# A hybrid decoder layer: where the rotary tables, the decays' sums, one row of the merged block and a few small steps stand

## The chip, the cores and the metric

The kernel runs on one core of one Trainium2 chip. The metric is the time of one execution on the device in microseconds; lower is better. The core has five engines with instruction queues of their own: TensorE multiplies matrices, VectorE and GpSimd do elementwise work, ScalarE does activations and copies, and SyncE (SP) only issues transfers here. Each engine takes its instructions strictly in order. Data lies in DRAM, in the on-chip SBUF (128 partitions), and, for the results of matmuls, in the banks of PSUM.

## The reference

One layer for 1024 tokens of width 1024, in float32: a norm, one wide projection, two token mixers side by side, their merge by gates, an output projection, a residual and a last norm.

```python
h = rms_norm(x, norm_w[layer])
proj = jnp.einsum('btd,de->bte', h, w_in[layer])
(a_q, a_k, a_v, a_gate, b_q, b_k, b_v, b_gate, b_low, m_a, m_b) = jnp.split(proj, offsets, axis=-1)

q = rope(a_q.reshape(bsz, t, A_HEADS, A_HEAD_DIM), positions)
k = rope(a_k.reshape(bsz, t, A_KV_HEADS, A_HEAD_DIM), positions)
v = a_v.reshape(bsz, t, A_KV_HEADS, A_HEAD_DIM)
o_a = sliding_window_attention(q, k, v, a_sinks[layer]) * jax.nn.silu(a_gate)
y_a = jnp.einsum('bte,ed->btd', o_a, w_a_proj[layer])

gk = jnp.einsum('btr,re->bte', b_low, b_gate_up[layer]) + b_gate_bias[layer]
log_a = jax.nn.log_sigmoid(gk.astype(jnp.float32)) / GATE_TAU
o_b = gated_linear_attention(b_q, b_k, b_v, log_a)
o_b = rms_norm(o_b, b_out_norm_w[layer]) * jax.nn.silu(b_gate)
y_b = jnp.einsum('bte,ed->btd', o_b, w_b_proj[layer])

merged = jax.nn.sigmoid(m_a) * y_a + jax.nn.sigmoid(m_b) * y_b
x = x + jnp.einsum('btd,de->bte', merged, w_out[layer])
return rms_norm(x, final_norm_w)
```

`rope` turns the first 32 and the last 32 columns of a head by angles position x frequency, and so needs a table of sines and one of cosines. `gated_linear_attention` multiplies queries by exp(b) and keys by exp(-b), where b is the running sum of `log_a` within a chunk.

## The kernel before

**Precision.** Every matmul operand is split into a high part (a cast to a shorter float format, on ScalarE) and a low part (the difference, on VectorE or GpSimd), and each product is made of three matmuls. For weights this is `split_w` (L116 to L118): `wh` on ScalarE, `wl` on the engine named by `rest[0]`, GpSimd for most of the kernel and VectorE at the start and at the end.

**Seven products.** The large projections use a scheme with seven half-size products in place of eight: `seven_products` (L455). It takes sums of weight blocks (L467 to L470, VectorE) and sums of the activations' blocks, which are made once: `tr` holds the raw sums t1 to t4 (L233 to L239), and `t_split` (L287) splits them (L292 on ScalarE, L293 on VectorE). The products' results are added up on VectorE (L489, L506, L531), and a function `emit` handles each finished block.

**The order of the work.** (1) `token_tile` loads a tile of 128 tokens, sums squares on ScalarE (L214), forms the scale on GpSimd (`rstd_of`, L144: L146 multiplies by 1/n and adds the epsilon, L147 raises to the power -0.5), applies scale and norm weights on VectorE (L220; the weights lie in two PSUM banks `nwb`, filled by a matmul with ones, L208), and transposes on TensorE with the identity `ident` (L224). (2) Four projections of the gate `m_a` (`m_half`, `m_tiles`, L250 and L332) and the rank-16 projection `low` (L355 to L365). (3) `pair` (L598) runs `seven_products` over pairs of column blocks: four pairs for `m_b`, each followed by `log_gate` (L576) for one head, then for the two halves of the heads the pairs for q and k of the linear attention, then its gate and its values. `log_gate` forms the running sums of the decays for one head and half of the tokens: three activations on ScalarE, and a minimum, a difference, a scan, a copy and a difference on VectorE; the result `gx` goes to DRAM (`sp_cum`, L595). When q and k are finished, `keep` (L616) loads that block back (L629), takes its exponential on ScalarE (L630) and multiplies on GpSimd (L631). The tiles for this come alternately from the pools `mwork` and `ex`, of two buffers each. (4) Window attention over 8 pairs of heads. (5) Linear attention (`gla`). (6) The projection of the first mixer (`ya`). (7) The projection of the second mixer, again as seven products, with the merge of the gates in `merge` (L1084), and the split of the merged blocks for the last projection in `sums` (L1051). (8) The output projection, the residual and the last norm (`norm`, `finish`).

**The rotary tables.** `rotary_tables` (L383) is a chain of 33 instructions on VectorE over tiles of 128 x 256 that reduces the angles to a turn, two sines on ScalarE (L420) and twelve stores to DRAM (L424). It is called behind the second pair of `m_b` and its log gates, with `issue_after(scan)`, which puts its VectorE instructions behind that scan.

**The merged blocks.** `mg` holds the merged blocks: c11, c12, c21 and c22 are its quarters, four rows (index k) of 128 x 512 each. The output projection's first product uses `mt[0]`, the split of c21, and so needs c21's row 3, which becomes ready with the sixth product of the last of four rounds (k = 3). `sums(6)` splits that row, then forms the sum row 3 (`sum_row(3)`: t1s = c22 - c21) and splits it into `mt[5]`. The merge of a block takes two loads and two VectorE instructions (L1090, L1091).

**What sets the order.** The program is written in the order above, and a planner that simulates the engines in time gives each engine its queue: of the instructions that it holds ready it takes the one that stands earliest in the text. `issue_after` adds a lower bound, `high_priority(offset=n)` puts what is under it n places earlier. Pools on the right side of SBUF are a stack: a pool that is opened after another was closed takes the same place and waits for the readers of what lay there.

## Time and profile before

| what | us |
|---|---|
| three timed runs | 1079.79, 1079.21, 1076.34 (median 1079.21) |
| the profiled execution | 1076.43 |
| its span, first to last instruction | 1074.6 |
| TensorE busy | 1027.0 (96%) |
| VectorE busy | 756.3 (70%) |
| ScalarE busy | 540.8 (50%) |
| GpSimd busy | 507.3 (47%) |
| moved by DMA | 140.54 MB, mean 131 GB/s |

The profile is of one execution. Busy time of TensorE counts the time in which a matmul was under way, at whatever clock; whether it keeps its pace is seen from the number of matmuls in a stretch. Idle time is put down to whatever released the engine last.

### The profile page before, as it was taken

What the parts mean: (1) busy time and instruction counts of PE and PEld (TensorE: products, weight loads), DVE (VectorE), ACT (ScalarE), POOL (GpSimd) and SP (SyncE); (2) the same over time, 40 slices, a digit from 0 to 9 for tenths busy, and PEclk for the clock granted to TensorE, in tenths of its full rate; (3) what the DMA queues carried; (4) which work ended last, traced back from release to release, by engine and by line L of the source; (5) the groups of instructions that cost most, each with busy time, mean ns of one, the idle gap of its engine ahead of it and who ended that gap; (6) DMA issues with size and microseconds to landing.
All of it is one profiled execution on the core that took longest, in us unless ns stands there. A gap on an engine that the chain in (4) does not pass through costs nothing.

```text
span 1074.6 us, 16232 instructions
## 1 busy us (share of the span) xinstructions
PE 1027.0 (96%) x5572; PEld 872.0 (81%) x5572; DVE 756.3 (70%) x1315; ACT 540.8 (50%) x1321; POOL 507.3 (47%) x438
## 2 busy tenths in 40 slices
PE   7999998989999999999999999989989999997996
PEld 5788866867889998888888888878778887786996
DVE  6984797444665332379988787878856388899786
ACT  6535576333343223466766667647655244244445
POOL 3034444778897444766678676747843100000002
PEclk9999999989999999999999999999999999999999
DMA  8413343444333317222222222429764388442415
GB/s 275 113 59 108 128 137 123 153 141 136 101 109 108 118 40 216 59 59 59 71 59 59 78 71 76 140 84 303 244 222 158 115 268 256 136 140 97 167 52 194
DMA packets 126260, 140.54 MB, mean 131 GB/s; under 512 B 10337, under 2 KB 87009, under 8 KB 126178
## 3 DMA queue, kind: packets, MB, share of 16 engines
q1 hardware_dynamic: 126178, 139.51, 41.1%
q8 instruction: 44, 0.72, 0.3%
q14 instruction: 38, 0.31, 0.1%
HBM read 94.52 MB, written 40.24 MB: 125 GB/s over the span
## 4 chain that ended last, share of the span: by engine, by line
PE 61%; DVE 9%; POOL 2%; ACT 2%; issue 2%; DMA 2%; SPq 0%; POOLq 0%; DVEq 0%; ACTq 0%
PE pj L134 25%; PE sj L134 13%; PE sj L452 13%; PE sc L765 2%; PE av L805 2%; PE av L849 2%; PE pt L789 1%; DVE b L978 1%; PE sc L849 1%; PE av L889 1%; DMA oraw<-sp_oa 1%; PE av L890 1%; PE pt L922 1%; DVE wl L118 1%; DVE sm L788 1%
## 5 line engine op out<-in xcount | busy, mean ns | idle before, releaser
L134 PE MATMUL pj<-o,wh 128*128 128x512 f32 x1072 | 348.2, 399 | 2.2 <-DVE o L228 1.6
L134 PEld LDWEIGHTS pj<-o,wh 128*128 128x128 f32 x1072 | 198.7, 190 | 42.9 <-DVE o L228 2.0
L134 PE MATMUL pj<-o,wl 128*128 128x512 f32 x536 | 213.2, 398 | 0.0
L118 POOL TENSOR_TENSOR wl<-sraw,wh 128x512 fp32r<-128x512 f32 (+1 forms) x98 | 155.5, 1604 | 111.8 <-ACT wh L117 105.1
L134 PEld LDWEIGHTS pj<-o,wl 128*128 128x128 f32 x536 | 101.1, 189 | 21.0
L134 PE MATMUL sj<-o,wh 128*128 128x512 f32 x352 | 111.2, 395 | 1.6 <-DVE o L489 0.8
L117 ACT CAST wh<-wr 128x1024 fp32r<-128x1024 f32 (+1 forms) x76 | 66.4, 890 | 78.4 <-PE sj L452 22.4
L117 ACT CAST wh<-sraw 128x512 fp32r<-128x512 f32 (+1 forms) x98 | 63.4, 678 | 83.7 <-PE sj L134 22.4
L146 POOL TENSOR_SCALAR rstd<-zs 128x1 f32<-128x1 f32 x8 | 2.7, 334 | 210.1 <-DVE zs L1110 209.7
L118 POOL TENSOR_TENSOR wl<-wr,wh 128x1024 fp32r<-128x1024 f32 x26 | 64.1, 2467 | 66.4 <-ACT wh L117 66.4
L506 DVE TENSOR_TENSOR u<-u,sj 128x512 f32<-128x512 f32 x48 | 32.9, 685 | 68.8 <-PE sj L134 35.6
L134 PEld LDWEIGHTS sj<-o,wh 128*128 128x128 f32 x352 | 65.7, 187 | 18.2 <-ACT u L515 1.3
L134 PE MATMUL sj<-o,wl 128*128 128x512 f32 x176 | 69.4, 394 | 0.0
L452 PE MATMUL sj<-wh,b 128*128 128x256 f32 x320 | 60.8, 291 | 6.0 <-DVE b L978 4.2
L134 PE MATMUL sj<-t,wh 128*128 128x512 f32 x144 | 57.6, 400 | 0.0
L489 DVE TENSOR_TENSOR c<-u,sj 128x512 f32<-128x512 f32 x48 | 32.7, 682 | 34.9 <-PE sj L134 10.5
L452 PEld LDWEIGHTS sj<-wh,b 128*128 128x128 f32 x320 | 51.8, 199 | 6.7 <-DVE b L978 4.4
L452 PE MATMUL sj<-wh,o 128*128 128x256 f32 x320 | 55.9, 278 | 1.3 <-DVE o L569 1.3
L780 ACT ACTIVATE sm<-sc,nm 128x129 f32<-128x129 f32 x128 | 45.8, 369 | 22.5 <-DVE nm L776 22.1
L797 POOL TENSOR_TENSOR ch<-ph,cst 128x512 fp32r<-128x512 f32 x32 | 37.1, 1158 | 40.4 <-ACT ph L796 32.9
L118 DVE TENSOR_TENSOR wl<-wr,wh 128x512 fp32r<-128x512 f32 (+1 forms) x50 | 45.4, 924 | 14.3 <-ACT wh L117 14.2
L452 PEld LDWEIGHTS sj<-wh,o 128*128 128x128 f32 x320 | 48.8, 188 | 1.6 <-DVE o L569 1.5
(316 smaller groups left out, 2707.0 us busy)
## 6 DMA issues: line engine op xcount, KB each, us to landing
sraw<-in_w_in_dram SPq DMA_DIRECT2D x32, 512.0 KB, 3.9
wr<-in_w_in_dram SPq DMA_DIRECT2D x26, 512.0 KB, 3.9
r<-sp_ob SPq DMA_DIRECT2D x28, 256.0 KB, 4.3
qs<-q SPq DMA_DIRECT2D x72, 64.0 KB, 2.0
xt<-in_x_dram SPq DMA_DIRECT2D x8, 512.0 KB, 8.1
sp_ma<-gt SPq DMA_DIRECT2D x16, 256.0 KB, 2.4
sp_mb<-c SPq DMA_DIRECT2D x16, 256.0 KB, 2.0
gt<-sp_cum SPq DMA_DIRECT2D x16, 256.0 KB, 3.4
```

What stands on the lines that cost most here:

```text
L117: nc.scalar.copy(h, raw)
L118: rest[0].tensor_sub(l, raw, h.bitcast(F32))
L134: nc.tensor.matmul(p, a[:, k, :], b[:, k, :], start=start and k == 0 and y == 0, skip_group_check=True, stop=stop and k == 3 and y == 2)
L452: nc.tensor.matmul(p, m[i][:, k, t * P : t * P + P], w[j][:, k, :], start=start and k == 0 and y == 0, skip_group_check=True, stop=stop an ...
L489: nc.vector.tensor_add(o, like(u[i][b], o), like(x[j][b], o))
L506: nc.vector.tensor_add(o[b], u[i][b], x[j][b])
L765: nc.tensor.matmul(s[:, h * 256 : h * 256 + 256], lq, kk[kv][x][:, k0 : k0 + 2, :].rearrange("p n t -> p (n t)"), start=x == 0, stop=x == 1)
L780: nc.scalar.activation(sm[:, j, :], sel[j // 2][:, j % 2, :], AF.Exp, bias=nm[:, j : j + 1], accum_out=den[:, j : j + 1])
L788: nc.vector.tensor_scalar_mul(sm[:, j, :P], sm[:, j, :P], den[:, j : j + 1])
L797: nc.gpsimd.tensor_mul(ch, ph.bitcast(F32), leb)
L805: nc.tensor.matmul(av[:, b * 256 : b * 256 + 256], val[:, blk, kv, :], part[:, 2 * b : 2 * b + 2, :], start=y == 0, stop=y == len(terms) - 1)
L849: nc.tensor.matmul(p, a[i], b[j], start=start and y == 0, stop=stop and y == 2)
```

## The change

Six edits:

1. `rotary_tables` is called right behind the splits of the t blocks and the last `m_a` tile, ahead of the pairs; `issue_after` puts its VectorE instructions behind the last split. Its pool `rt` moves from `gctx` to `tctx`, which closes there.
2. The decays' sums stay in SBUF: four tiles `cum` of 128 x 1024 take the place of the DRAM tile `sp_cum`. The eight stores and sixteen loads go, and so does the pool `ex`; the exponential reads `cum` and writes a tile of `mwork`.
3. In the last round of the second mixer's projection the merge and the split of c21's row 3 get a priority 400 places earlier; the merge of c22's row 3 is put off until behind that split, and the splits of c12 are put behind it as well.
4. The mean and the epsilon move out of `rstd_of`: the square takes a scale of D to the power -0.5, and the epsilon enters the sum as an extra column (of `xt` and of `ssq`). The first and the last norm so have one GpSimd instruction less for each tile; the linear attention's norm keeps it.
5. The norm weights and the identity are loaded through ScalarE's queue.
6. `low` is made ahead of the second halves of the first three `m_a` tiles and ahead of the t splits; the mask `caus` becomes a view of `le`, without the cast.

```diff
-    sp_cum = spill.tile([BH * BK, T], F32, name="sp_cum")
...
-    def rstd_of(pool, ss, n, width):
-        r = pool.tile([P, width], F32, name="rstd")
-        nc.gpsimd.tensor_scalar(r, ss, 1.0 / n, EPS, ALU.mult, ALU.add)
-        nc.gpsimd.tensor_tensor(r, r, mhalf[:, :width], ALU.pow)
+    def power(pool, ss):
+        r = pool.tile([P, 1], F32, name="rstd")
+        nc.gpsimd.tensor_tensor(r, ss, mhalf, ALU.pow)
         return r
...
-    rt = gctx.enter_context(pool_of(name="rt", bufs=1, side="right"))
...
     tctx = ExitStack()
+    rt = tctx.enter_context(pool_of(name="rt", bufs=1, side="right"))
     td = tctx.enter_context(pool_of(name="td", bufs=1, side="right"))
...
-        xts = [xp1.tile([P, D], F32, name=f"xt{t}") for t in range(NT)]
+        xts = [xp1.tile([P, D + 1], F32, name=f"xt{t}") for t in range(NT)]
+
+        for xt in xts:
+            nc.gpsimd.memset(xt[:, D:], (EPS * D) ** 0.5)
...
         load(0)
-        nc.sync.dma_start(cst[:, :P], consts[:, :P])
-        nc.sync.dma_start(nwr, norm_w)
+        nc.scalar.dma_start(nwr, norm_w)
+        nc.scalar.dma_start(cst[:, :P], consts[:, :P])
         load(1)
...
-            nc.scalar.activation(junk, xt, AF.Square, accum_out=ss)
-            r = rstd_of(xp, ss, D, 1)
+            nc.scalar.activation(junk, xt, AF.Square, scale=D**-0.5, accum_out=ss)
+            r = power(xp, ss)
...
+    last_split = []
...
-            nc.vector.tensor_sub(m[1][:, k, :], r[:, k, :], f(m, 0, k))
+            last_split.append(nc.vector.tensor_sub(m[1][:, k, :], r[:, k, :], f(m, 0, k)).ins)
...
-    for c in range(3):
-        m_half(c, w_first[c], 1)
-    t4, t2, t3, t1 = (t_split(*y) for y in ((4, None), (2, "t4"), (3, "t2"), (1, "t3")))
     low = lp.tile([P, T], F32R, name="low")
...
-    caus = const.tile([P, P], I32, name="caus")
-    nc.vector.tensor_copy(caus, le)
+    for c in range(3):
+        m_half(c, w_first[c], 1)
+    t4, t2, t3, t1 = (t_split(*y) for y in ((4, None), (2, "t4"), (3, "t2"), (1, "t3")))
+    caus = le.bitcast(I32)
...
     m_tiles([3])
-    rctx.close()
-    tctx.close()
-    c1.close()
...
+    with tc.issue_after(last_split[-1]):
+        rotary_tables()
+    rctx.close()
+    tctx.close()
+    c1.close()
...
-    decays = [mwork, sctx.enter_context(pool_of(name="ex", bufs=2))]
+    cums = gctx.enter_context(pool_of(name="cum", bufs=1, side="right"))
+    cum = [cums.tile([P, T], F32, name=f"cum{i}") for i in range(BH)]
...
-        gx = up_.tile([P, 512], F32, name="u3")
+        gx = cum[hd][:, sl]
...
-        nc.sync.dma_start(sp_cum[hd * BK : hd * BK + BK, sl], gx)
-        return scan.ins
...
-                decays.reverse()
-                t = decays[0].tile([P, 512], F32, name="gt")
-                r = row + a * P
-                nc.sync.dma_start(t, sp_cum[r : r + P, th * 512 : th * 512 + 512])
-                nc.scalar.activation(t, t, AF.Exp, scale=1.0 / 16.0 if mode == "up" else -1.0 / 16.0)
+                t = mwork.tile([P, 512], F32, name="gt")
+                nc.scalar.activation(t, cum[row // P + a][:, th * 512 : th * 512 + 512], AF.Exp, scale=1.0 / 16.0 if mode == "up" else -1.0 / 16.0)
...
-            scan = log_gate(c // 2, th)
-        if c == 2:
-            with tc.issue_after(scan):
-                rotary_tables()
+            log_gate(c // 2, th)
...
-        r = rstd_of(bp, ss, BV * BK, 1)
+        nc.gpsimd.tensor_scalar(ss, ss, 1.0 / (BV * BK), EPS, ALU.mult, ALU.add)
+        r = power(bp, ss)
...
-        nc.vector.tensor_sub(m[1][:, k, :], r, f(m, 0, k))
+        return nc.vector.tensor_sub(m[1][:, k, :], r, f(m, 0, k)).ins
...
+    first, late = [], []
...
         if i == 6:
-            split_block(mt[0], 3, c21[3])
+            with tc.high_priority(offset=400):
+                first.append(split_block(mt[0], 3, c21[3]))
+            with tc.issue_after(first[0]):
+                late.pop()()
             sum_row(3)
...
-            for k in range(4):
-                split_block(mt[6], k, c12[k])
+            with tc.issue_after(first[0]):
+                for k in range(4):
+                    split_block(mt[6], k, c12[k])
...
         def merge(o, a, th, b):
+            if (k, a, th) == (3, 1, 1):
+                late.append(lambda: merge_block(o, a, th))
+                return
+            with tc.high_priority(offset=400) if (k, a, th) == (3, 1, 0) else nullcontext():
+                merge_block(o, a, th)
+
+        def merge_block(o, a, th):
...
-    ssq = zw.tile([P, NT, 4], F32, name="ssq", bufs=1)
+    ssq = zw.tile([P, NT, 5], F32, name="ssq", bufs=1)
+    nc.gpsimd.memset(ssq[:, :, 4], EPS)
...
-        r = rstd_of(zw, ss, D, 1)
+        r = power(zw, ss)
...
-                nc.scalar.activation(junk, o[:, t, :], AF.Square, accum_out=ssq[:, tok, 2 * h + a : 2 * h + a + 1])
+                nc.scalar.activation(junk, o[:, t, :], AF.Square, scale=D**-0.5, accum_out=ssq[:, tok, 2 * h + a : 2 * h + a + 1])
```

8 lines of the change are left out of this document (4 added, 4 removed).

## The prediction

> **What bounds the kernel now.** I read the page first, then a table of busy time by stretch, then the waits and the timeline of each stretch that lost time. TensorE bounds the kernel, so a change is worth what it gives back of TensorE's lost time. The columns of the stretches: busy time of each engine with its count in brackets (PE is TensorE, DVE VectorE, ACT ScalarE, POOL GpSimd), granted clock, share of the DMA engines.
>
> ```profile
> core 0 of [0], span 1074.6 us
> core 0: us, PE busy (x) PEld busy (x) DVE busy (x) ACT busy (x) POOL busy (x), PEclk, DMA share, GB/s
> 80.00:130.00 50.00, 50.00 (x219) 40.79 (x218) 26.74 (x37) 28.71 (x48) 22.43 (x17) 1.00 0.37 116
> 140.00:250.00 110.00, 99.66 (x404) 77.85 (x403) 70.33 (x101) 55.34 (x89) 66.33 (x49) 0.95 0.45 142
> 200.00:250.00 50.00, 46.62 (x189) 36.94 (x188) 21.57 (x26) 17.81 (x32) 35.70 (x27) 0.93 0.53 165
> 250.00:300.00 50.00, 50.00 (x219) 40.69 (x218) 31.47 (x38) 18.43 (x32) 42.77 (x29) 1.00 0.28 92
> 980.00:1000.00 20.00, 15.27 (x103) 14.87 (x102) 20.00 (x30) 10.30 (x17) 0.00 (x0) 0.83 0.15 46
> 1000.00:1020.00 20.00, 20.00 (x169) 20.00 (x168) 13.38 (x19) 7.73 (x16) 0.00 (x0) 1.00 0.57 193
> ```
>
> From 80 to 130 and from 250 to 300 TensorE issues 219 matmuls in 50 us, 0.228 us each: its full pace. From 140 to 250 it issues 404, worth 92.2 us at that pace, so 17.8 us are lost; 6.9 of them (50 - 189 x 0.228) after 200, 10.9 before. Near the end the matmuls are 256 wide: 169 in 20 us is 0.118 us each, and 103 from 980 to 1000 are worth 12.2 us, so 7.8 are lost. VectorE is busy for all 20 us there. Busy shares hide this, as half-rate matmuls count as busy. The profiler may miss a few records, which would overstate these losses.
>
> The first loss follows the rotary tables. Timeline rows: start, length, engine, line, and in brackets the idle time before and who ended it.
>
> ```profile
> 166.75 0.42 ACT L420 ACTIVATE trig<-rad 128x256 f32<-128x256 f32 x1 [2.15 <-DVE rad L419]
> 167.08 0.61 ACT L117 CAST wh<-sraw 128x512 fp32r<-128x512 f32 x1
> ...
> 169.22 0.69 DVE L467 TENSOR_TENSOR sraw<-sraw 128x512 f32<-128x512 f32 x1 [1.18 <-POOL wl L118]
> ...
> 174.15 0.50 PE L134 MATMUL sj<-t2h,wh 128*128 128x512 f32 x1 [2.32 <-ACT wh L117]
> ```
>
> ScalarE stands in its queue 2.15 us for the second sine, because VectorE is late with the angle; only then does it cast a weight (L117), GpSimd splits it, VectorE waits 1.18 us for that split, and the next weight is cast late: TensorE idles 2.32 us. The other gaps up to 180 are of the same kind, smaller. The second loss, a row of the waits (total, times, longest) and then the timeline:
>
> ```profile
> ACT gt L630 <- DMA gt<-sp_cum: 25.3, 11, 4.7
> ...
> 208.71 0.63 ACT L630 ACTIVATE gt<-gt 128x512 f32<-128x512 f32 x1 [2.25 <-DMA gt<-sp_cum]
> 209.25 0.60 ACT L117 CAST wh<-sraw 128x512 fp32r<-128x512 f32 x1
> ...
> 211.25 1.76 DVE L467 TENSOR_TENSOR sraw<-sraw 128x512 f32<-128x512 f32 x1 [3.88 <-POOL wl L118]
> ...
> 222.13 0.80 PE L134 MATMUL sj<-t2h,wl 128*128 128x512 f32 x1 [2.27 <-POOL wl L118]
> 222.72 0.63 PE L134 MATMUL sj<-t2h,wh 128*128 128x512 f32 x1
> ...
> 227.84 0.49 PE L134 MATMUL sj<-t,wh 128*128 128x512 f32 x1
> ```
>
> ScalarE waits 25.3 us in all, 11 times, for sums read back from DRAM, each wait in front of casts: one of 2.25 us puts a cast at 209.25, and VectorE's L467, which needs GpSimd's split of it, idles 3.88 us until 211.25; behind the same chain TensorE idles 2.27 us and then runs 12 steps from 222.72 to 227.84 at 0.427 us, 2.4 us more than at full pace. One such stall costs 4.7 us. The third:
>
> ```profile
> 984.48 0.62 ACT L977 CAST b<-o 128x512 fp32r<-128x512 f32 x1 [0.56 <-DVE o L1091]
> ...
> 989.09 0.70 DVE L978 TENSOR_TENSOR b<-o,b 128x512 fp32r<-128x512 f32 x1
> ...
> 989.84 0.58 PE L452 MATMUL sj<-wh,b 128*128 128x256 f32 x1 [4.19 <-DVE b L978]
> ```
>
> The first product of the output projection lacks one block's low part (L978). ScalarE made the high part at 984.48; VectorE, with other work ahead of it, made the low part at 989.09; TensorE idled 4.19 us and then ran at half rate.
>
> **The change part by part.** *Rotary tables.* Their VectorE work runs from the row at 133.90 to the one at 166.43: 33 instructions, 15.6 us in all (10.9 if each took the shortest time of its line). The first three rows are the new place, the others what comes along.
>
> ```profile
> 66.19 3.61 DVE L293 TENSOR_TENSOR t<-t,t1h 128x512 fp32r<-128x512 f32 x4
> ...
> 86.02 0.69 DVE L489 TENSOR_TENSOR c<-u,sj 128x512 f32<-128x512 f32 x1 [10.05 <-PE sj L134]
> ...
> 91.41 0.69 DVE L506 TENSOR_TENSOR u<-u,sj 128x512 f32<-128x512 f32 x1 [4.70 <-PE sj L134]
> ...
> 133.90 0.26 DVE L385 CAST ang<-pos 128x256 f32<-128x256 int32 x1
> ...
> 162.89 1.28 ACT L420 ACT_TABLE_LOAD   x1
> ...
> 164.63 5.42 SPq L424 DMA_DIRECT2D sp_rope<-trig  x12
> ...
> 166.43 0.29 DVE L419 TENSOR_SCALAR rad<-rad 128x256 f32<-128x256 f32 x1
> ```
>
> They move behind the last split of the t blocks, which ends at 69.80. VectorE has 10.05 and 4.70 us idle there, against 10.9 to 15.6 us of work. The two sines and one or two table loads of 1.28 us go along, and twelve stores (5.42 us of SP's queue) now pass ahead of the first pair's stores and the second pair's weight loads. The nearest measure of those pairs without the tables is 80 to 130: full pace, with log gates too. So up to 10.9 us come back. What is late next is the log gate's own work on VectorE and GpSimd's splits. I take three quarters, 8.2, since the planner reorders the whole stretch and missing records flatter the loss; the cost at the new place lies between nothing (the idle time holds it) and the same 10.9 (the stall moves along); I take nothing, by the two idle rows.
>
> *Sums in SBUF.* Eight stores and sixteen loads of 256 KB go, with ScalarE's 25.3 us of waiting; the exponentials and GpSimd's multiplications stay. The nearest measure is 250 to 300, where pairs with as much GpSimd work (42.77 of 50 us) run at full pace. Up to 6.9 us; I take 5.2. The decays have two buffers where they had four, so a third exponential waits for GpSimd's first multiplication: between nothing and the rival below.
>
> *One row of merged first.* Its merge and split go ahead of VectorE's other work, and the merge of the neighbouring block goes behind. No instruction is removed. Its low part needs four VectorE steps (L489, L1090, L1091, L978) of some 0.7 us behind the product, so it could stand some 5 us sooner or more. Two bounds: nothing, since VectorE is full for all 20 us, and a product two places on, whose block needs the neighbour's merge that now goes behind, may wait instead; or all 7.8 us, since VectorE idles 6.6 us (20 - 13.38) in the next 20 and can do there what is put off. I take half, 3.9: no row is nearer to one end.
>
> *low made earlier.* Its matmuls now stand ahead of three products:
>
> ```profile
> 43.53 0.64 PE L134 MATMUL pj<-o,wh 128*128 128x512 f32 x1 [1.56 <-DVE o L228]
> ...
> 47.39 0.28 DVE L312 TENSOR_TENSOR lw<-lwr,lw 128x128 fp32r<-128x128 f32 x1
> ```
>
> Its weights are ready at 47.67, and TensorE already waits 1.56 us until 43.53. Put first too early, it would idle some 4 us more (43.53 to 47.67); put well, it fills nothing that is idle later. I take nothing, as the three products are ready first.
>
> *Start.*
>
> ```profile
> 1.16 0.42 SPq L198 DMA_DIRECT2D cst<-in_consts_dram  x1
> 1.62 0.33 SPq L199 DMA_DIRECT2D nwr<-in_norm_w_dram  x1
> 2.00 0.36 SPq L195 DMA_DIRECT2D xt<-in_x_dram  x1
> ...
> 4.15 3.75 PE L208 MATMUL av<-nwr,ones 1*128 1x512 f32 x4 [4.15 <-DMA nwr<-in_norm_w_dram]
> ...
> 5.54 0.19 POOL L146 TENSOR_SCALAR rstd<-ss 128x1 f32<-128x1 f32 x1 [4.10 <-ACT junk L214]
> ...
> 10.01 2.06 DVE L220 SCALAR_TENSOR_TENSOR xt<-xt,rstd,av 128x512 f32<-128x512 f32 x3 [2.85 <-POOL rstd L147]
> ```
>
> Each token's scale loses one GpSimd step (0.19 us, near 0.3 with the gap behind it); VectorE, which then works without a break, starts 2.85 us late at 10.01 behind that chain. The eight memsets of a column fall in GpSimd's 4.10 us of idle time, even at this step's 0.19 us each; one 128-wide cast goes, at most the 0.28 us of the like row at 47.39. With the two loads at 1.16 and 1.62 off SP's queue the second token's, at 2.00, is issued some 0.8 us earlier, but the norm weights, for which TensorE waited 4.15 us, now stand behind ScalarE's first work. Between 0.8 lost and 1.1 gained; I take 0.3. The Trainium skill, "DMA: Bandwidth & Descriptors", section "Issuing engines are not separate DMA queues", says that issuing from another engine only saves issue time and that the transfers share the same engines; by it the second queue's part of this is at most the issue time saved, and the sum stays within the same bounds. The first 10 us of the trace, with one queue in use, cannot show it.
>
> *End.*
>
> ```profile
> 1067.84 0.15 DVE L1110 TENSOR_REDUCE zs<-ssq 128x1 f32<-128x4 f32 x1
> ...
> 1068.43 0.48 POOL L146 TENSOR_SCALAR rstd<-zs 128x1 f32<-128x1 f32 x1
> 1068.99 0.55 POOL L147 TENSOR_TENSOR rstd<-rstd,mhalf 128x1 f32<-128x1 f32 x1
> ```
>
> The last four scales run one behind another on GpSimd, a step of 0.48 and one of 0.55 us each. The first goes. The last token's sum is there at 1067.99 (first row), so the power can start some 0.9 us before 1068.99, sooner still if the sums move up too: I take 1.0, between 0.3 (one token's step) and 1.4.
>
> Sum: 8.2 + 5.2 + 3.9 + 0.3 + 1.0 = 18.6. The profiled execution took 1076.4 (its span 1074.6 and 1.8 around it), which gives 1057.8; the median shown is 2.8 higher, 1079.2. I forecast 1059, between the two footings.
>
> **The rivals.**
> *Everything comes back*: 17.8 + 7.8 + 1.1 + 1.4 = 28.1, so 1048 to 1051. For it: the full pace on both sides. Against it: the planner's new order is unknown.
>
> *The stall moves, the change not doing what it says*: the tables, 33 dependent steps, delay the first pair's sums of weights, and ScalarE stands before a sine again. The 8.2 are given back, and VectorE's full load lets the merged row give nothing: 18.6 - 8.2 - 3.9 = 6.5, so about 1070. For it: 15.6 us of work into 14.8 us of gaps. At twice that price (another 8.2) the change ends at -1.7, no change. The Trainium skill, "SBUF — State Buffer", section "SBUF: two separate sides", has one exclusive port pair that VectorE and GpSimd take for whole instructions. By it the tables cost nearer 15.6 where GpSimd splits, which favours this rival; the trace agrees as far as 10.9 against 15.6 shows it.
>
> *Slower*: two decay buffers. An exponential waits in ScalarE's queue for GpSimd's multiplication, with casts behind it, so GpSimd's own splits come late in turn. If that makes a stall of 4.7 us twice in each of the four q and k pairs, it costs 37.6 instead of 6.9: 18.6 - 5.2 - 30.7 = -17.3, about 1094. It decides from the fifth stall on. For it: GpSimd is busy 35.70 of 50 us there. Against: the pairs from 250 on, fuller still, keep pace.
>
> **How the numbers follow.** The forecast, 1053 to 1066, gets 0.50; everything back 0.15; the stall moved 0.18; the same at twice its price 0.08; slower 0.09. About 0.3%, 3.2 us, is what a measurement can tell from no change. So faster is 0.50 + 0.15 + 0.18 = 0.83, same 0.08, slower 0.09. The range 1047 to 1072 takes in the first three.
>
> **What would show it.** Right: 219 matmuls per 50 us through 140 to 250; no table step there; the sine near 80 without TensorE idling; no wait on sums; the 4.19 us gone; four power steps alone at the end. Wrong: fewer than 219 in 70 to 120; ScalarE waiting on GpSimd between exponentials; TensorE idle before the output projection's third product; a later start than 10.01. All of it falls if the planner's new order costs time in the attention stage, where TensorE now keeps pace.

## The result, and the profile after

The changed kernel took 1062.88 us (median of four runs, 1061.71 to 1065.27), the kernel before 1077.78 us beside it (1074.71 to 1079.79): a ratio of 0.9867, with a 95% interval of 0.9835 to 0.9899. That is 3.8 us above the 1059 forecast, inside the range of 1047 to 1072 and inside the likeliest case's own 1053 to 1066. The profiled execution took 1061.71 us with a span of 1059.9, so the spans differ by 14.7 us, where the sum of the prediction had 18.6.

First the busy time by stretch, of the kernel before (one row that the prediction did not need) and of the changed kernel, with the columns explained there.

```profile
core 0 of [0], span 1074.6 us
...
0.00:50.00 50.00, 39.89 (x187) 31.76 (x188) 39.03 (x68) 28.82 (x51) 8.32 (x23) 0.97 0.67 208
```

```profile
core 0 of [0], span 1059.9 us
...
0.00:50.00 50.00, 44.18 (x218) 35.23 (x219) 42.09 (x70) 30.92 (x55) 8.69 (x24) 0.97 0.69 214
50.00:100.00 50.00, 50.00 (x218) 40.60 (x217) 42.90 (x72) 25.64 (x44) 16.84 (x13) 1.00 0.28 84
140.00:200.00 60.00, 56.21 (x243) 45.01 (x242) 39.80 (x51) 32.27 (x53) 37.69 (x27) 1.00 0.32 104
200.00:250.00 50.00, 48.65 (x212) 39.44 (x211) 26.26 (x30) 20.01 (x36) 42.19 (x30) 1.00 0.37 118
950.00:980.00 30.00, 20.96 (x131) 18.01 (x131) 30.00 (x45) 15.73 (x27) 0.11 (x1) 0.94 0.24 77
```

Between 140 and 250 TensorE now issues 455 matmuls where it issued 404. The stretch from 50 to 100 holds the rotary tables (VectorE 42.90 us busy in place of some 32) and still runs at the full 218. But there are two things that the prediction did not have: the first 50 us gained 31 matmuls, and at 950 to 980 nine microseconds of TensorE are idle.

Stretches of equal length hold different work in two kernels, so I then set the traces side by side at equal work. Both record the same number of matmuls, 5572. Each is given an issue time at full pace by its shape, taken from the traces (0.230 us for 512 columns, 0.117 for 256, 0.084 for 128, 0.06 or 0.11 for 64, and 0.85 for each of the four one-row matmuls at the start), 978.7 us in all; the time that has passed beyond that sum at the same place is TensorE's lost time. The stretches are cut where 100, 185, 250, 825 and 975 us of this work are done. The same place is the same amount of work, and where the change alters the order not always the same matmul. Two pairs of rows show the reading. The same softmax transpose and the same matmul of the last product, before and after:

```profile
486.92 0.55 PE L789 MATMUL pt<-cst,sm 128*128 128x128 f32 x3 [1.10 <-DVE pl L798]
...
1064.19 0.50 PE L452 MATMUL sj<-wh,o 128*128 128x256 f32 x2 [1.32 <-DVE o L569]
```

```profile
469.64 0.44 PE L787 MATMUL pt<-cst,sm 128*128 128x128 f32 x2 [1.10 <-DVE pl L796]
...
1049.08 0.50 PE L456 MATMUL sj<-wh,o 128*128 128x256 f32 x2 [1.10 <-DVE o L573]
```

At the first the changed kernel is 17.28 us ahead, at the second 15.11. So more than 2 us were lost again behind the attention. By stretches (named by the work done, with the kernel's own clock beside it), TensorE's lost time is:

| stretch | before: until | lost | after: until | lost | gained | the prediction's term |
|---|---|---|---|---|---|---|
| start: tokens, first gate | 119.9 | 19.9 | 112.8 | 12.8 | 7.2 | start 0.3, low 0 |
| tables: gate m_b and log gates | 215.4 | 10.5 | 203.5 | 5.7 | 4.8 | tables 8.2 |
| sums: queries and keys | 287.3 | 6.9 | 270.1 | 1.6 | 5.4 | sums 5.2 |
| middle: to the second mixer's projection | 897.7 | 35.3 | 880.4 | 35.4 | -0.1 | none |
| last: merge, output projection | 1060.4 | 12.8 | 1045.6 | 15.1 | -2.3 | merged row 3.9 |
| last matmuls | 1065.5 | 1.4 | 1050.5 | 1.3 | 0.2 | none |
| tail: behind the last matmul | 1074.6 | 9.1 | 1059.9 | 9.5 | -0.4 | end 1.0 |

These add up to the 14.7 us of the spans, within rounding. Only the sums came out at the size forecast; the start gave 24 times its term, the tables just over half, and the merged row and the end came out with the other sign, both by less than such stretches differ between runs (see e9 and the tail).

### The profile page after: what moved, and what is told of

It is laid out like the page before. It is cut to its first block, busy times and chain, and to the rows that moved or that the text cites. A ratio compares the mean times of both kernels' runs of the same rounds, so it can differ in the third digit from the quotient of the medians.

```text
span 1059.9 us, 16193 instructions
## 1 busy us (share of the span) xinstructions
PE 1017.9 (96%) x5572; PEld 868.0 (82%) x5572; DVE 754.9 (71%) x1314; ACT 538.8 (51%) x1319; POOL 502.5 (47%) x431
## 4 chain that ended last, share of the span: by engine, by line
PE 63%; DVE 7%; POOL 4%; DMA 3%; issue 2%; ACT 2%; SPq 0%; POOLq 0%; DVEq 0%; ACTq 0%
PE pj L133 25%; PE sj L133 16%; PE sj L456 13%; PE sc L763 2%; PE av L803 2%; PE av L847 2%; DMA r<-sp_ob 1%; DVE b L977 1%; PE pt L787 1%; PE sc L847 1%; PE av L887 1%; PE av L888 1%; DVE wl L117 1%; PE pt L921 1%; POOL wl L117 1%
## 5 line engine op out<-in xcount | busy, mean ns | idle before, releaser
L510 DVE TENSOR_TENSOR u<-u,sj 128x512 f32<-128x512 f32 x48 | 32.9, 685 | 61.9 <-PE sj L456 32.7
L456 PE MATMUL sj<-wh,b 128*128 128x256 f32 x320 | 58.5, 284 | 1.0 <-ACT wh L116 0.8
L133 PE MATMUL sj<-b,wh 128*128 128x512 f32 x160 | 49.5, 393 | 1.3 <-ACT wh L116 1.1
```

The costliest lines, as they stand in the source:

```text
L133: nc.tensor.matmul(p, a[:, k, :], b[:, k, :], start=start and k == 0 and y == 0, skip_group_check=True, stop=stop and k == 3 and y == 2)
L456: nc.tensor.matmul(p, m[i][:, k, t * P : t * P + P], w[j][:, k, :], start=start and k == 0 and y == 0, skip_group_check=True, stop=stop an ...
L510: nc.vector.tensor_add(o[b], u[i][b], x[j][b])
```

## The experiments

All of them are edits of the changed kernel, and every ratio is against the kernel before, run beside it on the same chip. The last column is the stretch table for each run's profiled execution; "start" to "last" are TensorE's lost microseconds as above.

| run | median us | ratio, 95% interval | start | tables | sums | middle | last |
|---|---|---|---|---|---|---|---|
| kernel before | 1077.78 | | 19.9 | 10.5 | 6.9 | 35.3 | 12.8 |
| changed kernel | 1062.88 | 0.9867 (0.9835 to 0.9899) | 12.8 | 5.7 | 1.6 | 35.4 | 15.1 |
| e1 merged row in its old turn | 1063.69 | 0.9859 (0.9830 to 0.9889) | 12.4 | 5.9 | 1.4 | 33.6 | 18.4 |
| e2 low behind the splits | 1061.67 | 0.9833 (0.9801 to 0.9866) | 12.6 | 4.3 | 1.5 | 35.4 | 16.6 |
| e3 both loads on SP's queue | 1067.17 | 0.9899 (0.9870 to 0.9928) | 18.8 | 2.7 | 1.3 | 36.1 | 18.1 |
| e4 scale in two steps | 1063.21 | 0.9855 (0.9825 to 0.9885) | 17.9 | 3.6 | 1.4 | 32.7 | 15.5 |
| e5 sums in DRAM | 1071.33 | 0.9938 (0.9914 to 0.9961) | 12.3 | 7.3 | 7.8 | 36.5 | 18.9 |
| e6 sums in DRAM, tables back | 1075.47 | 0.9979 (0.9959 to 0.9998) | 13.0 | 11.0 | 6.2 | 41.5 | 19.1 |
| e7 weight sums on GpSimd | 1064.22 | 0.9868 (0.9841 to 0.9896) | 12.8 | 5.7 | 1.8 | 38.9 | 17.9 |
| e8 weight sums and splits on GpSimd | 1074.75 | 0.9971 (0.9950 to 0.9993) | 12.8 | 5.9 | 1.6 | 39.1 | 30.6 |
| e9 changed kernel again | 1063.78 | 0.9863 (0.9844 to 0.9881) | 12.2 | 5.9 | 1.4 | 37.5 | 18.3 |
| e10 low late, two queues at the end | 1058.73 | 0.9827 (0.9802 to 0.9852) | 13.0 | 4.5 | 1.4 | 35.4 | 19.7 |
| e11 multiplication on VectorE | 1061.51 | 0.9855 (0.9834 to 0.9876) | 12.7 | 6.8 | -0.1 | 31.9 | 15.4 |
| e12 the three edits of e10 and e11 | 1061.24 | 0.9843 (0.9828 to 0.9859) | 13.0 | 5.4 | -0.1 | 37.2 | 15.2 |

### e9: how far one order differs from run to run

> The changed kernel itself, unaltered, beside the next three on the same chip: 1061 to 1065 by its four runs so far. Its stretches against the same matmuls of the first profile tell how much a stretch differs from run to run with one and the same order of instructions: by the theory that the experiments so far are told apart by their stretches, less than 1 us in each, and in the gated attention stage, where runs differed by up to 4 us, up to that.

It is the same program as the changed kernel. Its first three stretches repeat within 0.6 us. Its middle lost 2.1 more and its last stretch 3.2 more, so the expectation of less than 1 us outside the gated attention was wrong for the last one. In the last stretch most of the difference lies at one wait that is in both; first the changed kernel's first profile, then this one:

```profile
895.49 0.74 PE L133 MATMUL sj<-b,wh 128*128 128x512 f32 x2 [1.14 <-ACT wh L116]
```

```profile
898.58 0.73 PE L133 MATMUL sj<-b,wh 128*128 128x512 f32 x2 [2.68 <-ACT wh L116]
```

and the stretch around it, in e9:

```profile
880.00:900.00 20.00, 17.32 (x75) 13.76 (x74) 18.33 (x31) 10.60 (x20) 0.00 (x0) 0.99 0.84 266
```

The matmul waits for a weight's cast, and ScalarE's queue has casts of blocks read back from DRAM there, with the DMA engines 84% busy; for one such block ScalarE waits 1.70 us in e9 (until 893.05) and 0.26 in the first profile (until 890.32). A wait of 1.14 us costs about that; the one of 2.68 is followed by six matmuls at half rate. So in what follows, differences of under 1 us in the first three stretches are not used, and of under some 4 us in the middle and the last stretch neither, unless a row names their cause.

### e3 and e4: where the start's 7.2 us come from

```diff
e3:
-        nc.scalar.dma_start(nwr, norm_w)
-        nc.scalar.dma_start(cst[:, :P], consts[:, :P])
+        nc.sync.dma_start(cst[:, :P], consts[:, :P])
+        nc.sync.dma_start(nwr, norm_w)
e4:
-            nc.scalar.activation(junk, xt, AF.Square, scale=D**-0.5, accum_out=ss)
+            nc.scalar.activation(junk[:, :D], xt[:, :D], AF.Square, accum_out=ss)
+            nc.gpsimd.tensor_scalar(ss, ss, 1.0 / D, EPS, ALU.mult, ALU.add)
             r = power(xp, ss)
```

> The changed kernel with the norm weights and the identity loaded from SyncE's queue behind the first token, in the order of before. The prediction put this part between 0.8 lost and 1.1 gained. Theory A: the queue gives the 1.2 us by which the first matmul starts sooner and part of the 2.1 us by which the second token is there sooner, and with it the 4.0 us near 40 us: 1065 to 1069. Theory B: the first stage waits for GpSimd and VectorE, not for the loads: within 0.7 us of 1063.

> The changed kernel with each token's scale in two GpSimd steps again (multiply and add, then the power; the tail keeps one step). Theory A (the prediction's term): some 0.3 us at the first token only, so 1063. Theory B: the step counts once for every token, 8 times 0.28, and pushes the last tokens behind the planner's products: 1065 to 1067, with the idle time near 40 us back.

Each of the two brings the lost time of the start back nearly whole: 18.8 and 17.9 us, against 12.8 with both and 19.9 before. Timeline rows of ScalarE's square of the second token, before, after, and with the loads back on SP's queue:

```profile
7.91 1.06 ACT L214 ACTIVATE junk<-xt 128x1024 f32<-128x1024 f32 x1 [2.46 <-DMA xt<-in_x_dram]
```

```profile
6.05 1.06 ACT L215 ACTIVATE junk<-xt 128x1025 f32<-128x1025 f32 x1 [0.30 <-DMA xt<-in_x_dram]
```

```profile
7.41 1.06 ACT L215 ACTIVATE junk<-xt 128x1025 f32<-128x1025 f32 x1 [1.83 <-DMA xt<-in_x_dram]
```

The queue alone is worth 1.36 us at the second token (7.41 - 6.05), not the 0.8 of saved issue time, and TensorE's first matmul moves from 4.77 to 2.95. The norm weights, which the prediction saw behind ScalarE's first work, are issued at 0.73 (1.62 before), ahead of it:

```profile
0.73 0.52 ACTq L199 DMA_DIRECT2D nwr<-in_norm_w_dram  x1
```

But the larger part, 4.0 us, is the hole near 40 us whose row the prediction quoted (43.53, idle 1.56). In the changed kernel it is gone; with either edit undone it is there again. Timeline rows of TensorE: the changed kernel, then e3, then e4.

```profile
35.91 0.60 PE L225 MATMUL pt<-cst,xt 128*128 128x128 f32 x4
36.35 1.04 PE L225 MATMUL sc<-cst,xt 128*128 128x128 f32 x8
37.29 1.22 PE L133 MATMUL pj<-o,wh 128*128 128x512 f32 x3
```

```profile
42.48 0.79 PE L133 MATMUL pj<-o,wh 128*128 128x512 f32 x1 [2.05 <-DVE o L229]
43.08 0.63 PE L133 MATMUL pj<-o,wl 128*128 128x512 f32 x1
```

```profile
39.41 0.73 PE L133 MATMUL pj<-o,wh 128*128 128x512 f32 x2 [0.66 <-ACT o L229]
...
41.70 0.79 PE L133 MATMUL pj<-o,wh 128*128 128x512 f32 x1 [1.56 <-DVE o L230]
42.29 0.63 PE L133 MATMUL pj<-o,wl 128*128 128x512 f32 x1
```

In the changed kernel the last transposes stand at 35.91, one `pt` block and two `sc` blocks, and the products run on at 37.29 without a wait. In the others TensorE waits for VectorE's split of those blocks and then runs at half rate. The planner places the transposes by the time at which it expects the tokens, and either delay changes that place: as these rows read, the hole is there whole or not at all, and is no sum of small savings. At the start it is theory A of e3 and theory B of e4. Yet e4's median is only 0.3 us above the changed kernel's, below the 1065 to 1067 that theory B expected, and e3's is 4.3 above (3.4 by the ratios, whose intervals overlap: for e3 too it is the stretches that show the effect). Part of the answer is in the table: where TensorE starts late, the stretch of the tables loses less (2.7 and 3.6 against 5.7), because the other engines are further ahead of it there: in e3 TensorE enters the stretch at 118.8 in place of 112.8, 6.0 us later, but VectorE's first scan starts only 2.8 us later (104.2 and 101.4). So 2 to 3 us of the start's gain are given back in the next stretch. The rest of e4's difference lies in the middle, which e9 shows to be too uncertain to explain.

### e2: the low-rank product

```diff
-    low = lp.tile([P, T], F32R, name="low")
-    ...
     for c in range(3):
         m_half(c, w_first[c], 1)
     t4, t2, t3, t1 = (t_split(*y) for y in ((4, None), (2, "t4"), (3, "t2"), (1, "t3")))
+    low = lp.tile([P, T], F32R, name="low")
+    ...
     caus = le.bitcast(I32)
```

> The changed kernel with the low-rank product of the gate behind the splits of the t blocks again, as before. The prediction gave its move nothing. Theory A: the 4.0 us that the changed kernel is ahead between the third product of the first stage and the second (where the kernel before idled 1.56 us and then ran 12 matmuls at half rate) come from this move: some 1067, and the idle time near 40 us is back. Theory B: they come from the earlier tokens (queue and rstd): within 0.7 us of 1063.

The start doesn't move (12.6), so theory B: the product's place has no part in the hole near 40. The stretch of the tables loses 1.4 us less than the changed kernel (4.3 against 5.7): a wait of 0.86 us at 130.10, for ScalarE's copy behind a log gate, is in the changed kernel and not in e2. Why it is gone there the rows don't tell: the log gates' scans stand 1.6 to 2.6 us earlier in e2, but for one. So this part of the change costs a little, where it was taken at nothing. By the whole time, 1061.67 against 1062.88, it can't be told apart.

### e5 and e6: the sums and the tables

```diff
e5 (the sums' pool goes, the two pools of two decay buffers come back):
-        gx = cum[hd][:, sl]
+        gx = up_.tile([P, 512], F32, name="u3")
+        nc.sync.dma_start(sp_cum[hd * BK : hd * BK + BK, sl], gx)
-                t = mwork.tile([P, 512], F32, name="gt")
-                nc.scalar.activation(t, cum[row // P + a][:, th * 512 : th * 512 + 512], AF.Exp, ...)
+                decays.reverse()
+                t = decays[0].tile([P, 512], F32, name="gt")
+                nc.sync.dma_start(t, sp_cum[r : r + P, th * 512 : th * 512 + 512])
+                nc.scalar.activation(t, t, AF.Exp, ...)
e6, as well (and the pool of the tables goes back to `gctx`):
-    with tc.issue_after(last_split[-1]):
-        rotary_tables()
+        if c == 2:
+            with tc.issue_after(scan):
+                rotary_tables()
```

> The changed kernel with the sums of the decays written to DRAM and read back again, with four decay buffers; the rotary tables stay at their new place. Theory A (the prediction's term, and the 5.4 us by which the changed kernel draws ahead between 205 and 262 us of before): 5 us come back as waits of ScalarE for the read-back, some 1068, and TensorE's 2.3 us gap with 12 half-rate steps near 200 us is back. Theory B: the waits only changed their name (ScalarE now waits 28.6 us for GpSimd's multiplications where it waited 25.3 us for the read-back), and what was gained there came from the tables' place: within 1 us of 1063.

> As the kernel with the sums in DRAM, and the rotary tables back behind the second pair's log gate as well (with the sums in SBUF the tables' room isn't there at that place, so the two can't be undone one without the other in that order). Against the run with the sums alone in DRAM this prices the tables. Theory A (the prediction's term): 8.2 us more, some 1076. Theory B (from matching matmuls): only 4.8 to 6 us more, 1073 to 1074, because the log gates' own scans, exponentials and splits stall TensorE there without the tables too (1.0, 1.5, 1.6, 1.1 us at 130 to 174 us in the changed kernel). Theory C: the tables at their new place cost as much as at the old: within 1 us of the run with the sums alone.

Undoing the sums costs 8.5 us by the medians (7.7 by the ratios, each against its own kernel before) and 6.2 in their own stretch (7.8 against 1.6), so theory A. The waits of ScalarE, of the changed kernel (145 to 255 us) and of e5 (145 to 275; over its whole run 28.6 us, 12 times), and TensorE's in e5:

```profile
ACT gt L631 <- POOL c L632: 28.6, 11, 4.4
```

```profile
ACT gt L635 <- DMA gt<-sp_cum: 24.2, 9, 5.2
```

```profile
207.92 0.50 PE L134 MATMUL sj<-t3h,wl 128*128 128x512 f32 x1 [0.96 <-POOL wl L118]
...
211.62 0.79 PE L134 MATMUL sj<-t2h,wl 128*128 128x512 f32 x1 [2.25 <-POOL wl L118]
```

ScalarE waits as long in the one as in the other, only for GpSimd instead of a transfer. What differs is what the wait does: with the read-back TensorE's gap of 2.25 us is there again (last fence, e5). Why the waits for GpSimd cost TensorE so little is not shown; a likely reason is that GpSimd, which makes the splits that TensorE needs, goes on working while ScalarE waits for it. The wait's total said nothing of its price.

The tables cost 4.1 us by the medians of e6 and e5 (1075.47 - 1071.33) and 3.7 in their stretch (11.0 - 7.3): theory B, somewhat less (the time itself, 1075.47, is near theory A's 1076, but only because e5 came out above the 1068 expected of it). The two intervals just touch. With the tables gone from it the stretch still loses 4.3 (e2) to 7.3 us (e5) where TensorE starts early, and 2.7 and 3.6 where it starts late (e3, e4). Rows of the changed kernel there, TensorE and what held ScalarE's copy:

```profile
128.74 1.29 DVE L599 TENSOR_TENSOR cum<-u,cend 128x512 f32<-128x512 f32 x2
...
129.47 1.07 ACT L519 COPY u<-sj 128x512 f32<-128x512 f32 x2 [5.01 <-DVE cum L599]
...
130.10 0.73 PE L133 MATMUL sj<-o,wh 128*128 128x512 f32 x2 [0.86 <-ACT u L519]
```

A log gate alone does it: two scans of 2.2 us and their last differences on VectorE, ScalarE's copy of a PSUM bank behind them after 5.01 us of idle time, TensorE without a bank. Two more waits of this kind (1.38 us until 151.52, 0.97 until 174.28) and one of 1.44 us for GpSimd's split of a weight (until 165.29) make up nearly all that this stretch still loses. In the kernel before, the tables' work lay on top of this.

### e1: the merged row in its old turn

```diff
-            with tc.high_priority(offset=400):
-                first.append(split_block(mt[0], 3, c21[3]))
-            with tc.issue_after(first[0]):
-                late.pop()()
+            split_block(mt[0], 3, c21[3])
...
-            with tc.issue_after(first[0]):
-                for k in range(4):
-                    split_block(mt[6], k, c12[k])
+            for k in range(4):
+                split_block(mt[6], k, c12[k])
...
-            if (k, a, th) == (3, 1, 1):
-                late.append(lambda: merge_block(o, a, th))
-                return
-            with tc.high_priority(offset=400) if (k, a, th) == (3, 1, 0) else nullcontext():
-                merge_block(o, a, th)
+            merge_block(o, a, th)
```

> The changed kernel, with the one row of merged made in its old turn (no priority, the neighbour's merge not put off). It took 1062.9 us beside 1077.8 of the kernel before. Theory A (the prediction's, half of it): the priority gives 3.9 us, so without it the time is some 1066 to 1067. Theory B (from matching the same matmuls in the two traces): of the 17.2 us that the change is ahead at the middle of the last stage, 2.3 are lost again by its end, because the priority lets the weights of the output projection be summed and split late; without it the time is some 1060 to 1061, and the long wait of TensorE is the 4 us one for the low part again. Theory C: the planner makes much the same loss either way, within 1 us of 1063.

Theory C: 1063.69 against 1062.88 and 1063.78. Timeline rows of the changed kernel: TensorE's two waits in the output projection, and the steps of VectorE and ScalarE that they wait for.

```profile
973.65 1.24 DVE L471 TENSOR_TENSOR wr<-wr 128x1024 f32<-128x1024 f32 x1
...
974.98 1.05 ACT L116 CAST wh<-wr 128x1024 fp32r<-128x1024 f32 x1 [1.29 <-DVE wr L471]
...
976.08 0.89 PE L456 MATMUL sj<-wh,o 128*128 128x256 f32 x4 [3.65 <-ACT wh L116]
...
978.32 1.24 DVE L117 TENSOR_TENSOR wl<-wr,wh 128x1024 fp32r<-128x1024 f32 x1
...
979.62 0.58 PE L456 MATMUL sj<-wl,o 128*128 128x256 f32 x1 [2.66 <-DVE wl L117]
```

And TensorE in e1:

```profile
969.33 0.39 PE L456 MATMUL sj<-wh,b 128*128 128x256 f32 x1 [0.65 <-DVE b L977]
...
976.35 1.22 PE L456 MATMUL sj<-wh,o 128*128 128x256 f32 x4 [3.41 <-ACT wh L116]
...
979.90 0.58 PE L456 MATMUL sj<-wl,o 128*128 128x256 f32 x1 [2.33 <-DVE wl L117]
```

The wait of 4.19 us for the row is gone in the changed kernel (0.22 is left at 967.86), but also, but for 0.65 us, without the priority, because the planner orders this whole stretch differently now: it is not the priority that removes it. In its place TensorE waits twice for the third product's weights, the sum that VectorE makes at 973.65 and its low part at 978.32, with the priority and without. The half clock that follows is in the stretch too: between the same places on both sides of these waits (from 960 to 985 us in the changed kernel) the changed kernel loses 9.5 us, e9, the same program, 9.6, and the kernel before, around its one wait, 8.5. Without the priority, in e1, it is 11.2; but e3, which keeps the priority, loses 11.0 there too. So the priority may be worth up to some 1.7 us at this place, which is not shown, and the 3.9 that it was to bring are not there. Of the 2.3 us by which the whole last stretch loses more than before, 1.0 lies here and 1.1 ahead of it, where e9 differs from the same program by 3.1.

### e7 and e8: less work for VectorE there

```diff
e7:
-        nc.vector.tensor_add(a22, a21, a22)
+        sums_on[0].tensor_add(a22, a21, a22)
...  (and so the other three sums)
     for h in range(2):
+        sums_on[0] = nc.vector if h else nc.gpsimd
e8, as well:
+        rest[0] = nc.vector if h else nc.gpsimd
```

> The changed kernel with the four sums of raw output weights of the output projection's first half made by GpSimd, which is idle from 833 to 1047 us but for one memset, in place of VectorE, which is full from 950 to 980. Theory A: VectorE's load, not the turn of one row, bounds this stretch; TensorE's two waits of 3.65 and 2.66 us are for weights that VectorE sums (the sum at 973.65, its cast at 974.98, the split at 978.32), and 4 sums of 1.24 us off VectorE bring 2 to 5 us: 1058 to 1061. Theory B: GpSimd needs twice as long for each and holds VectorE up meanwhile, or TensorE then waits for the row again: within 1 us of 1063 or slower.

> As the last, and GpSimd makes the low parts of that half's seven weight tiles too (2.46 us each there, 1.23 on VectorE). Theory A: 13.6 us of work off VectorE in all; the stretch from 950 to 985, which loses 9.5 us, loses 2 to 5 instead: 1056 to 1060. Theory B: seven splits of 2.46 us in GpSimd's order come later than VectorE's would, TensorE waits for them: 1063 or slower.

Theory B in both: 1064.22, no gain, and 1074.75, a loss of some 11 us. The rows say why. GpSimd, then VectorE, then TensorE, in e7, and last GpSimd in e8:

```profile
975.16 7.54 POOL L472 TENSOR_TENSOR wr<-wr 128x1024 f32<-128x1024 f32 x1 [137.59 <-DVE wl L118]
982.77 2.37 POOL L473 TENSOR_TENSOR wr<-wr 128x1024 f32<-128x1024 f32 x1
```

```profile
979.79 0.71 DVE L1051 TENSOR_TENSOR o<-o,o 128x512 f32<-128x512 f32 x1
983.80 2.42 DVE L118 TENSOR_TENSOR wl<-wr,wh 128x1024 fp32r<-128x1024 f32 x1 [3.31 <-ACT wh L117]
```

```profile
983.83 1.23 PE L457 MATMUL sj<-wh,o 128*128 128x256 f32 x4 [7.06 <-ACT wh L117]
```

```profile
957.16 12.62 POOL L118 TENSOR_TENSOR wl<-wr,wh 128x1024 fp32r<-128x1024 f32 x2 [119.43 <-ACT wh L117]
```

The sum was to take some 2.4 us. It lasted 7.54, because VectorE ran without a break until 980.50; it ended 2.2 us after that, and the next sum, beside an idle VectorE, took 2.37. Then VectorE's split, 1.24 us elsewhere, took 2.42 beside GpSimd. TensorE waited 7.06 us for this weight's cast. In e8 GpSimd's first two splits took 12.62 us together. So moving these sums and splits from the full VectorE to GpSimd brought nothing here. Whether VectorE's load or the planner's order bounds this stretch is therefore not told apart by these runs: the work could not be made lighter.

### e10 to e12: the tail, the decay buffers, and a version beyond both

```diff
e10 (with the edit of e2):
-        nc.sync.dma_start(out[t * P : (t + 1) * P, :512], z0)
+        nc.scalar.dma_start(out[t * P : (t + 1) * P, :512], z0)
e11:
-                nc.gpsimd.tensor_mul(c, c, t)
+                nc.vector.tensor_mul(c, c, t)
```

> The changed kernel with two edits: the low-rank product behind the splits again (alone it gave 1061.7, and TensorE lost 1.7 us less up to 210 us), and the first half of each token's output stored from ScalarE's queue, the second from SyncE's as now. In the changed kernel the last calculation ends 3.97 us behind the last matmul's start (4.78 before), but the span ends 9.4 behind it (9.1 before), and SyncE's queue issues its last stores one behind another, 0.6 us each. Theory A: the tail's gain was given back in that queue, and two queues bring 0.5 to 1.2 us: with low's 1 to 1.7, 1060 to 1062. Theory B: the end hangs on the last transfer's own time, or ScalarE's issues delay its last scales: no gain or a loss from the second edit, 1061.5 to 1063.

> The changed kernel with the multiplication by the decay made by VectorE instead of GpSimd, so that a decay buffer comes free sooner and GpSimd only splits there. ScalarE waits 28.6 us for these multiplications between 145 and 255 us. Theory A (the rival of the prediction, two decay buffers paced by GpSimd): the waits cost TensorE what it still loses there, 1.6 us at 208 (and what the planner left for them); they go, and 1 to 2 us with them: 1061 to 1062. Theory B: they stand beside TensorE's work and cost nothing, VectorE is as late as GpSimd was: within 1 us of 1063.

> The three edits of the last two runs together. If each is worth what its stretch shows, 1058.5 to 1061.5; if the planner's order gives the early gains back later, as it did with the start, 1061 to 1063.

*The tail.* In the changed kernel the scales come as forecast: no multiply-and-add steps, and the last calculation starts at 1054.10, 3.6 us behind the last matmul (1050.48), where it started 4.4 behind before. But the first of the last eight stores is issued 1.3 us behind the last matmul in both kernels, and from there the DMA engines are 88 and 91% busy and the last four stores land some 0.7 us apart, in both kernels. SP's queue and the stretch behind it, before, then the same two after:

```profile
1066.89 0.33 SPq L1114 DMA_DIRECT2D out_dram<-o  x1
```

```profile
1067.00:1072.00 5.00, 0.00 (x0) 0.00 (x0) 2.31 (x8) 2.34 (x5) 2.21 (x5) 0.91 0.88 324
```

```profile
1051.77 0.33 SPq L1128 DMA_DIRECT2D out_dram<-o  x1
```

```profile
1052.00:1057.00 5.00, 0.00 (x0) 0.00 (x0) 2.16 (x7) 2.20 (x5) 1.49 (x2) 0.80 0.91 336
```

Eight stores of 256 KB at 336 GB/s are 6.2 us. That, more than the scales, makes the end: 7.7 us from the first of these issues to the end of the span before, 8.1 after. The second queue brings the tail from 9.5 to 9.0 us in e10 and e12, but e3 and e4 have 9.0 with one queue too, so no gain of its own is shown for it, and the 0.4 us by which the tail grew is no more than runs differ. The Trainium skill, "DMA: Bandwidth & Descriptors", section "Issuing engines are not separate DMA queues", has all queues run on the same DMA engines, a second one saving issue time alone; the tail agrees.

*The decay buffers.* With the multiplication on VectorE, TensorE loses nothing at all in the stretch of the sums (-0.1 against 1.4 to 1.6), but 0.9 to 1.1 more in the stretch before, part of which is the same pairs begun earlier. The net is some 0.6 us. So the two decay buffers cost at most the 1.6 us of that stretch, and the times (1061.51 beside 1063.78, intervals overlapping) can't tell theory A from theory B. No run has four decay buffers beside the sums in SBUF.

*A version beyond both.* e10 has the lowest median, 1058.73, against 1063.78 for the changed kernel on the same chip. The intervals overlap (0.9802 to 0.9852, 0.9844 to 0.9881), the stretches explain some 2 us of the 5, and e12, with one edit more, has 1061.24. That e10 beats the changed kernel is likely but not shown; both beat the kernel before.

## Why the prediction came out as it did

The sign, the size and the likeliest case were right, but the sum was right by errors that cancel, which is luck: 18.6 forecast, 14.7 measured, with 6.9 too little at the start and 11 too much in the tables, the row and the tail together, as the stretches divide it.

**Sums in SBUF** (5.2 forecast): right, 5.4 in the stretch, and 6.2 in the stretch or 7.7 to 8.5 in all when undone alone. The nearest measure chosen, the pairs from 250 on with as much GpSimd work at full pace, was a good one.

**Tables** (8.2): the mechanism is right, the size not. The new place costs nothing (218 matmuls from 50 to 100, as the two idle rows suggested), although the 33 steps took 17.3 us there, from 69.01 to 88.86, and not less than the 15.6 of their old place; so neither rival in which the stall moves along with the tables came true. The step that failed is "three quarters of 10.9". It put TensorE's whole loss between 140 and 200 down to the tables; the log gates next to them, and a weight's split, still cost 2.7 to 7.3 us there without the tables, as the rows of ScalarE's copy behind VectorE's scans show in part in the profile after; with the early start of the changed kernel the tables are worth 3.7 to 4.8. How much depends on the start: in e3 and e4, which start nearly as late as the kernel before, the stretch loses 7.8 and 6.9 us less than before, some of it by the sums. No run moves the tables alone out of the kernel before, so how start and tables share their common gain stays open. The measure taken for "pairs without the tables", 80 to 130 at full pace, held the first pairs only.

**Merged row** (3.9): wrong. The step that failed is "I take half". Its lower bound, nothing, had the right reason, that VectorE is full for all 20 us, and the half taken had none. The wait of 4.19 us does go, but the planner's new order removes it without the priority too, but for 0.65 us (e1). What is late next was named in a general way, a product two places on, and listed as a sign of being wrong, and is so: the third product waits 3.65 and 2.66 us in place of the 4.19 for the row, for its weights and not for the neighbour's merge. The part of the second rival in which the row gives nothing is what happened; the part with the tables is not.

**Low earlier** (0): off by 1.4 us in the stretch of the tables, a loss in these profiles; too small to see in the whole time.

**Start** (0.3, between 0.8 lost and 1.1 gained): wrong by the largest amount: 7.2 us in its stretch, of which 2 to 3 are given back in the next. Three steps failed. The loss allowed for, norm weights behind ScalarE's first work, didn't come: their load is issued ahead of that work. The saved issue time of 0.8 us was taken for the gain at the second token, where the token came 1.86 us sooner. The rule of the Trainium skill that the prediction cites for this part, that a queue saves issue time alone, was no bound there: with the loads back on SP's queue that square starts 1.36 us later, more than the 0.84 us by which the token's own issue is then later; the two transfers also stand ahead of the token's again, but no run separates that share. And the 1.56 us of idle time at 43.53, quoted for the low-rank product, was never followed back to the tokens. It and its half-rate matmuls are 4.0 us that hang on the tokens' times by way of the planner, and both small edits, the queue and the shorter scale, were needed to remove them.

**End** (1.0): the chain of scales is 0.8 us shorter, near the forecast; the step that failed is that this chain was taken for the end. The eight stores behind it were already the bound.

**Slower by two decay buffers**: not seen. ScalarE does wait for GpSimd between exponentials, 28.6 us, the very sign that the prediction listed as wrong, and TensorE loses 1.6 us for it at most. The row that spoke against that rival, the pairs from 250 on, decided rightly.

**The attention stage** kept its pace through the new order, as the forecast needed (35.3 and 35.4 us lost in the middle).

## What to carry to other kernels

Set two traces side by side at equal work, not at equal time, before a gain is put down to an edit: here the whole was right to 4 us while four of six parts were not. Follow every gap of the bounding engine back to its first cause, also those that the change seems not to touch, because with a planned order a quarter of a microsecond for each token can bring back a gap of four. And before a wait is removed in a stretch where an engine is full, name the next work in that engine's queue and its due time: that is where the wait goes.

## What the runs showed of the hardware

VectorE and GpSimd hold each other up much more than their separate durations tell. Beside a VectorE that ran two-input steps back to back, a GpSimd sum of 2.37 us lasted 7.54 and two splits 12.62, and VectorE's split of 1.24 lasted 2.42 beside GpSimd, ending 1.1 us behind GpSimd's sum. The Trainium skill, "SBUF — State Buffer", section "SBUF: two separate sides", describes an exclusive pair of ports that the two take for whole instructions. The exclusion agrees; that GpSimd, recorded from 975.16, let some five microseconds of VectorE's steps pass, most of them begun after it, before its own 2.2 us is more than one instruction's turn. VectorE's step at 974.98 was the earlier one, and its steps follow 0.60 us apart at 0.70 us each; whether the ports came free between them the trace does not show.

TensorE fell to half rate (0.427 us for a matmul of 512 columns in place of 0.23) behind a single wait of 2.68 us (e9, 898.58), behind 2.05 us that began 0.7 us after one of 0.39 (e3, 42.48), behind 2.66 us that began 0.9 us after one of 3.65 (changed kernel, 979.62), and also behind 1.56 us that began 0.7 us after one of 0.66 (e4, 41.70); after single waits of 0.86 and 1.14 us (changed kernel, 130.10 and 895.49) it did not.
